# Out-projection stores of a two-layer encoder trunk, issued from POOL's queue in place of SP's

## The chip, the cores and the metric

The kernel runs on one core of a Trainium2 chip. Its engines are named as in the profile: PE is TensorE (matmuls; PEld are its weight loads), DVE is VectorE, ACT is ScalarE, POOL is GpSimd, and SP is SyncE, which here only issues DMAs. Each engine works through its own instructions in order. An instruction that waits (for another engine's result, for a buffer, for a DMA to land) holds up all that stand behind it on the same engine. A DMA is issued by one engine's queue and then carried out by 16 DMA engines that all queues share. The metric is device time in microseconds (us). Before the change the median of three runs is 2117.21 us (2113.16 to 2118.84).

## The reference, cut to what matters

A trunk of two layers works on 1024 tokens with 16 learned tokens in front (1040), 1024 channels, in float32. Each layer normalises, projects to four head groups of 512 channels (pooling, 2-D Fourier, bidirectional state-space scan "SSD", grouped-query attention), gates each, and projects the concatenation back:

```python
def reference(x, meta_tokens, norm_w, w_in, w_out, ...):
    h = jnp.concatenate([meta, x], axis=1)
    for i in range(DEPTH):
        hn = rmsnorm(h, norm_w[i])
        proj = jnp.einsum("bld,de->ble", hn, w_in[i])
        ...
        y_pool = multiscale_pool(u_pool, ...) * jax.nn.silu(g_pool)
        y_fft = fourier_mix(u_fft, fourier_w[i]) * jax.nn.silu(g_fft)
        y_ssd = ssd_mixer(xbc, z, dt_raw, ...)
        y_att = gqa_axial(q, k, v, ...) * jax.nn.silu(g_attn)
        mixed = jnp.concatenate([y_pool, y_fft, y_ssd, y_att], axis=-1)
        h = h + jnp.einsum("ble,ed->bld", mixed, w_out[i])
    return h[:, N_META:]
```

The last product, with `w_out`, is the out-projection. The change is in the code that adds its results to `h` and stores them.

## The kernel before, in words

All activations stand channel by channel: 128 channels on the partitions, tokens along the row, cut into three chunks (348, 346 and 346 tokens; in the second layer the first chunk loses the 16 learned tokens and has 332). For float32 accuracy each operand is split into a high part (cast on ACT, L128) and a low part (subtraction on DVE, L129), and each product takes three matmuls (L132, L133, L134).

The out-projection is not one product over 2048 channels. It is made in four passes, one per group of 512 channels, as soon as the group is ready: `outproj` is called for group 0 (pooling), then 1 (Fourier), then 3 (attention), then 2 (SSD, called the tail). Each pass reads `h` plus what earlier passes added from DRAM (hidden tensors, `hd` in the profile, or the input `xT`), adds its part, and writes the sum back to DRAM for the next pass; the last pass of the last layer writes `out`.

One pass has 8 blocks of 128 output channels times 3 chunks, 24 items. An item does this:

- SP loads the block of `h` to a small tile `ht` (L338). These tiles (`sms` in the profile) come from a ring of four buffers, which other steps use too: spilled projections (L239, L240), loads of group results (L325), the accumulator of the SSD's end (L950).
- TensorE makes 12 matmuls to a PSUM bank (`psmm`, or a spare bank `psy`).
- DVE adds the bank to `ht` in place (L352). In the attention group's pass (`pool=True`) ACT copies the bank to a second small tile (L349) and POOL adds (L350). In the tail of the first layer the sum goes to a tile that stays on chip as well (`sink`), since it is the next layer's input.
- SP stores the sum (L353).

That makes 24 stores for each of four groups and two layers, 192 in all. Once per block SP also loads the weights (L205, a ring of four buffers), which ACT and DVE split.

The passes don't run by themselves. Items are woven between the steps of other stages: the attention's last part (POOL adds to `acc` at L663 and L665), `fft_tables`, `fft_inner` (its inputs are loaded at L443 and L455, POOL clears tiles at L453 and L480), `fft_outer`, the gates, the SSD. How many items go to which stage is set by hand (the tables `FB`, `FW`, `TW`). The tile framework then schedules each engine's instructions from this program, so that a change of one instruction's engine can move others.

`fft_outer` matters for the change. It makes four sets of four matmul groups, each group with six matmuls against a cosine or sine table and one more at L518. POOL issues the DMA of each set's table (L499), and of one small table before (L493). The results of the first and third set are copied by ACT (L522), those of the second and fourth are combined by DVE (L524, L525). The gates are loaded by SP at L312, and ACT applies their silu at L306, ahead of the third set's copies. After this stage the SSD begins, with products at L790 and loads at L830 and L835.

Of the kernel before, what the change touches and what calls it, by code (L numbers as in the profile page):

```python
# [52 lines left out]
def hybrid_trunk(ctx: ExitStack, tc: tile.TileContext, io, out, depth=DEPTH):  # L53
    nc = tc.nc
# [42 lines left out]
    def big(dt=F32):  # L97
        return bigp.tile([128, SLOT], dt, name=nm("big"), tag="big", bufs=NBIG)
# [3 lines left out]
    def sm(tag="n", dt=F32):  # L102
        pool = phase["p"] if tag == "q" else smp
        return pool.tile([128, 348], dt, name=nm("sm" + tag), tag="sm" + tag, bufs=phase["q"] if tag == "q" else SMB[tag])
# [12 lines left out]
    def ps(tag):  # L117

        ring = [tag] * PSB[tag] + [x for x, t in zip(("y0", "y1", "y2"), phase["spare"]) if t == tag]
        turn[tag] = (turn[tag] + 1) % len(ring)  # L120
        x = ring[turn[tag]]
        return psp.tile([128, 512], F32, name=nm("ps" + x), tag=x, bufs=PSB.get(x, 1))
# [8 lines left out]
    def mm3(out_ps, ah, al, bh, bl, start, stop):  # L131
        nc.tensor.matmul(out_ps, ah, bh, start=start, stop=False)  # L132
        nc.tensor.matmul(out_ps, ah, bl, start=False, stop=False)  # L133
        nc.tensor.matmul(out_ps, al, bh, start=False, stop=stop)  # L134
# [58 lines left out]
    def wsplit(raws, cols=128):  # L193

        r = []
        for raw in raws:
            wh = wp.tile([128, 4, 128], F32R, name=nm("wh"), tag="wh", bufs=WB[1])
            wl = wp.tile([128, 4, 128], F32R, name=nm("wl"), tag="wl", bufs=WB[1])
            split(wh[:, :, :cols], wl[:, :, :cols], raw)
            r += [(wh[:, k, :cols], wl[:, k, :cols]) for k in range(4)]  # L200
        return r

    def wraw(src, cols=128):
        w = wp.tile([128, 4, 128], F32, name=nm("wr"), tag="wr", bufs=WB[0])
        nc.sync.dma_start(w[:, :, :cols], src)  # L205
        return w[:, :, :cols]
# [123 lines left out]
    def outproj(l, s, g, mixed, src, dst, chunks=(0, 1, 2), pool=False, sink=None):  # L330

        part = mixed()
        for d in range(8):
            w = wsplit([wraw(io["w2"][l, g, d])])
            for ci in chunks:
                c0, cw = s.ch[ci]
                ht = sm("s")[:, :cw]
                nc.sync.dma_start(ht, src(d, ci)[:, -cw:])  # L338
                p = ps("mm")
                for k in range(4):  # L340
                    mm3(p[:, :cw], *w[k], part(s, 0, k, ci), part(s, 1, k, ci), k == 0, k == 3)
                o = ht
                if sink is not None:
                    if len(sink) == d:
                        sink.append(big())
                    o = sink[d][:, c0:c0 + cw]
                if pool:
                    t = sm("s")[:, :cw]
                    nc.scalar.copy(t, p[:, :cw])  # L349
                    nc.gpsimd.tensor_tensor(o, ht, t, op=ALU.add)  # L350
                else:
                    nc.vector.tensor_tensor(o, ht, p[:, :cw], op=ALU.add)  # L352
                nc.sync.dma_start(dst(d, ci)[:, -cw:], o)  # L353
                yield


# [662 lines left out]
    for l in range(depth):  # L1019
# [29 lines left out]
        def early():  # L1049

            s.pm = load_mixed(s, "p")
            for _ in range(GP):
                yield
        fill2 = chain(early(), outproj(l, s, 0, lambda: s.pm, hsrc, d0), outproj(l, s, 1, lambda: s.fm, d0, d2), outproj(l, s, 3, lambda: s.am, d2, d1, pool=True))
        main = att_main(l, s, 3)
        run(weave((islice(main, LS + 3 * PC - 1), LS + 3 * PC - 1), (chain(*side), PS), (chain(fill, islice(fill2, GP + FB[0])), WF * (n + GP + FB[0]))))
# [23 lines left out]
        hsrc = by_rows(out, NM) if last else hidden()  # L1080
        sink = None if last else []
        tail = lambda chunks: outproj(l, s, 2, lambda: ssd_parts(s, chunks), d1, hsrc, chunks, sink=sink)
        fwd = ssd_fwd(l, s)
        n = 48 - FB[6] - FB[7]
# [119 lines left out]
```

## Time and profile before

| | before |
|---|---|
| runs, us | 2113.16, 2117.21, 2118.84 |
| profiled execution: own time | 2113.91 us |
| profiled execution: span in the profile | 2112.0 us |
| granted TensorE clock, mean | 0.981 |
| TensorE busy | 94% of the span |
| DVE, ACT, POOL busy | 66%, 48%, 17% |
| DMA packets of POOL's queue (software_dynamic), share of 16 engines | 1.7% |
| DMA packets of the other issuers' queue (hardware_dynamic) | 38.9% |

The span is the time between the first and the last instruction that the profiler recorded; the execution's own time is 1.9 us longer. A row such as `PE psmm L132 <- DVE sms L352: 9.2, 11, 2.1` reads: TensorE, at its instruction on line 132 that writes a tile `psmm`, stood for 9.2 us in 11 cases, at most 2.1 us, until DVE's instruction on line 352 that writes a tile `sms` had ended. `SPq` is SP's queue of DMA issues. Line 352 is the add, 353 the store, 338 the load of `h`. The clock column of the stage rows is the TensorE clock that was granted in that window as a share of full speed.

### The profile page before, as it was taken

Reading aid. Unit: us, or ns where it says so; the run is one execution under the profiler, and the core shown is the slowest. Engines: PE = TensorE matmul, PEld = TensorE weight load, DVE = VectorE, ACT = ScalarE, POOL = GpSimd, SP = SyncE. Lnnn points to the kernel's source line nnn. Section 1 sums busy time; section 2 is a strip of 40 time slices with the busy share of each in tenths; the row PEclk is TensorE's granted clock in tenths of the full one; section 3 lists DMA queues with packets and bytes.
Section 4 is the critical chain, followed back from the end, with each engine's and each line's share of the span. In section 5 each row is a group of like instructions: output and inputs, shape, how many; then the busy total and the mean of one; then the engine's idle time right before and its main releaser. Section 6 shows DMA issues by size and latency. Waiting matters only on the chain. (4 is left out here: it accounts for less than half of the span.)

```text
span 2112.0 us, 33087 instructions
## 1 busy us (share of the span) xinstructions
PE 1991.0 (94%) x11880; PEld 1744.1 (83%) x11880; DVE 1397.0 (66%) x2693; ACT 1012.7 (48%) x2192; POOL 369.0 (17%) x365
## 2 busy tenths in 40 slices
PE   6999999999999998998789999999999999989988
PEld 4898988688899777887779988876888995878877
DVE  5675546767665555799785755476676636477985
ACT  5544344453543546356465343436535425463562
POOL 2012122032120300013120121221312203000330
PEclk9999999999999998999899999999999999989999
DMA  4321221123232567766644221122122335877766
GB/s 139 101 75 60 67 65 57 42 74 98 92 126 97 172 207 234 203 182 186 176 123 121 68 67 55 59 61 69 65 96 98 116 117 153 248 219 198 195 180 182
DMA packets 164666, 260.99 MB, mean 124 GB/s; under 512 B 20938, under 2 KB 113678, under 8 KB 164502
## 3 DMA queue, kind: packets, MB, share of 16 engines
q1 hardware_dynamic: 161846, 249.56, 38.9%
q0 software_dynamic: 2656, 9.33, 1.7%
q8 instruction: 93, 1.52, 0.3%
q14 instruction: 71, 0.58, 0.1%
HBM read 182.92 MB, written 71.67 MB: 121 GB/s over the span
## 5 line engine op out<-in xcount | busy, mean ns | idle before, releaser
L132 PE MATMUL psmm<-big,wh 128*128 128x346 f32 (+2 forms) x1920 | 643.9, 336 | 35.3 <-ACT sms L349 12.7
L133 PE MATMUL psmm<-big,wh 128*128 128x346 f32 (+2 forms) x1920 | 628.7, 327 | 8.7 <-DVE big L129 5.6
L134 PE MATMUL psmm<-big,wl 128*128 128x346 f32 (+2 forms) x1920 | 624.6, 326 | 2.6 <-DVE wl L129 2.6
L132 PEld LDWEIGHTS psmm<-big,wh 128*128 128x128 f32 x1920 | 368.5, 192 | 84.5 <-issue 31.8
L133 PEld LDWEIGHTS psmm<-big,wh 128*128 128x128 f32 x1920 | 368.4, 192 | 17.9 <-DVE big L129 7.9
L134 PEld LDWEIGHTS psmm<-big,wl 128*128 128x128 f32 x1920 | 368.5, 192 | 5.9 <-DVE wl L129 4.3
L665 POOL TENSOR_TENSOR acc<-acc,pf 116x346 f32<-116x346 f32 (+5 forms) x216 | 221.0, 1036 | 672.9 <-ACT pf L655 537.9
L128 ACT CAST wh<-wr 128x512 fp32r<-128x512 f32 (+1 forms) x236 | 145.1, 616 | 265.2 <-PE psmm L133 182.7
L129 DVE TENSOR_TENSOR wl<-wr,wh 128x512 fp32r<-128x512 f32 x232 | 162.0, 703 | 123.0 <-ACT wh L128 121.8
L132 PE MATMUL psy<-big,wh 128*128 128x346 f32 (+2 forms) x672 | 221.2, 329 | 3.2 <-ACT big L128 2.5
L133 PE MATMUL psy<-big,wh 128*128 128x346 f32 (+2 forms) x672 | 217.3, 323 | 3.1 <-DVE big L188 2.0
L134 PE MATMUL psy<-big,wl 128*128 128x346 f32 (+2 forms) x672 | 216.5, 322 | 0.0
L655 ACT ACTIVATE pf<-psy 116x346 f32<-116x346 f32 (+4 forms) x288 | 125.4, 457 | 89.4 <-PE psy L653 88.2
L675 PE MATMUL pspv<-pf,vt 116*64 116x346 f32 (+5 forms) x864 | 165.5, 465 | 0.0
L665 DVE TENSOR_TENSOR acc<-acc,pf 116x346 f32<-116x346 f32 (+5 forms) x120 | 109.3, 911 | 75.5 <-ACT pf L655 51.0
L624 DVE TENSOR_REDUCE mx<-psy 116x1 f32<-116x346 f32 (+3 forms) x272 | 132.7, 511 | 17.3 <-PE psy L623 16.9
L132 PEld LDWEIGHTS psy<-big,wh 128*128 128x128 f32 x672 | 126.6, 188 | 15.2 <-issue 7.4
L133 PEld LDWEIGHTS psy<-big,wh 128*128 128x128 f32 x672 | 126.6, 188 | 6.9 <-DVE big L188 3.1
L134 PEld LDWEIGHTS psy<-big,wl 128*128 128x128 f32 x672 | 126.7, 189 | 0.8
L350 POOL TENSOR_TENSOR sms<-sms,sms 128x346 f32<-128x346 f32 (+2 forms) x48 | 61.9, 1292 | 355.3 <-DMA bb<-csd 230.6
L675 PEld LDWEIGHTS pspv<-pf,vt 116*64 116x64 f32 (+1 forms) x864 | 59.0, 136 | 61.7 <-issue 26.0
L352 DVE TENSOR_TENSOR sms<-sms,psmm 128x346 f32<-128x346 f32 (+2 forms) x104 | 52.8, 509 | 73.5 <-PE psmm L134 37.6
(293 smaller groups left out, 3273.0 us busy)
## 6 DMA issues: line engine op xcount, KB each, us to landing
wr<-w SPq DMA_DIRECT2D x248, 256.0 KB
sms<-hd SPq DMA_DIRECT2D x112, 173.0 KB
hd<-sms SPq DMA_DIRECT2D x96, 173.0 KB
bb<-csd SPq DMA_DIRECT2D x40, 338.0 KB
md<-big SPq DMA_DIRECT2D x24, 520.0 KB
gd<-sms SPq DMA_DIRECT2D x64, 173.0 KB
big<-gd SPq DMA_DIRECT2D x16, 520.0 KB
big<-md SPq DMA_DIRECT2D x16, 520.0 KB
```

Source lines behind the costliest of these rows:

```text
L128: nc.scalar.copy(hi, src)
L129: nc.vector.tensor_tensor(lo, src, f(hi), op=ALU.subtract)
L132: nc.tensor.matmul(out_ps, ah, bh, start=start, stop=False)
L133: nc.tensor.matmul(out_ps, ah, bl, start=False, stop=False)
L134: nc.tensor.matmul(out_ps, al, bh, start=False, stop=stop)
L350: nc.gpsimd.tensor_tensor(o, ht, t, op=ALU.add)
L352: nc.vector.tensor_tensor(o, ht, p[:, :cw], op=ALU.add)
L624: nc.vector.tensor_reduce(mx[:qn, q, e, ci:ci + 1], p[:qn, :cw], axis=AX.X, op=ALU.max)
L655: nc.scalar.activation(pf[:n, :cw], p[:n, :cw], AF.Exp, scale=0.125)
L665: eng.tensor_tensor(accs[c0, e][:n, :cw], accs[c0, e][:n, :cw], pf[:n, :cw], op=ALU.add)
L675: nc.tensor.matmul(hold["pv"][64 * e:64 * e + 64, :cw], s.vt[:n, k, v, :], pfs[e][:n, :cw], start=(k == 0), stop=(k == len(KTS) - 1))
```

## The change

One word changes in `outproj`: the store is issued from POOL's queue.

```diff
                 else:
                     nc.vector.tensor_tensor(o, ht, p[:, :cw], op=ALU.add)
-                nc.sync.dma_start(dst(d, ci)[:, -cw:], o)
+                nc.gpsimd.dma_start(dst(d, ci)[:, -cw:], o)
                 yield
```

All 192 stores move from SP's to POOL's queue, where each waits for its add. The scheduler then orders the other instructions anew. The numbers behind tile names tell tiles apart: an item's small tile, its bank and its sum have numbers close to each other.

On SP in the last tail (second layer, group 2), a piece of the difference: L338 loads `h` for an item, L205 loads weights, L893 loads a table of the SSD.

```order
 L205 DMA wr_21526<-w 128x512
 L338 DMA sms_21372<-hd_16517 128x346
 L205 DMA wr_21578<-w 128x512
-L353 DMA out<-sms_21315 128x332
 L205 DMA wr_21601<-w 128x512
-L353 DMA out<-sms_21332 128x346
-L353 DMA out<-sms_21355 128x332
 L338 DMA sms_21437<-hd_16516 128x332
-L353 DMA out<-sms_21372 128x346
 L338 DMA sms_21454<-hd_16517 128x346
```

The stores leave the queue, and the loads and weight loads stand directly behind each other.

On POOL in the first layer's Fourier stage, a piece of the difference: L493 and L499 are the tables of `fft_outer` (the tile 7973 is the second set's, 8051 the third's, 8123 the fourth's), L353 the stores of group 0.

```order
 L493 DMA big_7916<-dw 96x1048
 L499 DMA big_7918<-dl 128x1048
+L353 DMA hd_5729<-sms_8106 128x346
+L353 DMA hd_5727<-sms_8151 128x348
+L353 DMA hd_5728<-sms_8222 128x346
 L499 DMA big_7973<-dl 128x1048
+L353 DMA hd_5729<-sms_8259 128x346
+L353 DMA hd_5727<-sms_8282 128x348
 L499 DMA big_8051<-dl 128x1048
 L499 DMA big_8123<-dl 128x1048
```

The second set's table now stands behind three stores, the third's behind two more. The order in the second layer is alike.

On TensorE the items stand elsewhere around these sets. Before, the second set's first matmuls (`psxx_7975`) come after nine matmuls of the item with the bank 8261:

```order
L134 MATMUL psmm_8261<-big_7142,wl_8148 128x346
L132 MATMUL psmm_8261<-big_7143,wh_8147 128x346
L133 MATMUL psmm_8261<-big_7147,wh_8147 128x346
L134 MATMUL psmm_8261<-big_7143,wl_8148 128x346
L132 MATMUL psxx_7975<-big_7973,big_7871 128x262
L133 MATMUL psxx_7975<-big_7973,big_7871 128x262
```

Now they come after all of the next item's:

```order
L134 MATMUL psmm_8284<-big_7143,wl_8279 128x348
L132 MATMUL psmm_8284<-big_7144,wh_8278 128x348
L133 MATMUL psmm_8284<-big_7148,wh_8278 128x348
L134 MATMUL psmm_8284<-big_7144,wl_8279 128x348
L132 MATMUL psxx_7975<-big_7973,big_7871 128x262
L133 MATMUL psxx_7975<-big_7973,big_7871 128x262
```

Items stand about one item earlier against the transform's sets than before. In the order after, TensorE makes the whole item with the bank `psy_8224` (its sum is stored from the small tile 8222), one matmul of 8261, the first set, the other 11 of 8261, the 12 of 8284 (stored from 8282), the second set, ten of the next item, and the third set.

## The prediction

> **What bounds the kernel now.** I read the page's busy table first, then what TensorE waited for, then what SP's queue waited for, then the same waits stage by stage.
>
> ```profile
> PE 1991.0 (94%) x11880; PEld 1744.1 (83%) x11880; DVE 1397.0 (66%) x2693; ACT 1012.7 (48%) x2192; POOL 369.0 (17%) x365
> ```
>
> TensorE is busy for 1991 of 2112 us, so a change that leaves the matmuls alone can only win from the 121 us in which it stands. The waits of TensorE (line that waits, what ended it, total us, times, longest):
>
> ```profile
> PE psmm L132 <- ACT sms L349: 12.7, 11, 3.1
> PE psy L132 <- ACT big L522: 9.3, 2, 4.7
> PE psmm L132 <- DVE sms L352: 9.2, 11, 2.1
> ...
> PE psy L790 <- DVE sms L352: 4.0, 1, 4.0
> ...
> PE psmm L132 <- DVE big L352: 1.8, 2, 1.1
> ```
>
> L352 and L349 read an out-projection's sum out of PSUM. While they are late no bank comes free and TensorE stops. The four rows that name them make 12.7 + 9.2 + 4.0 + 1.8 = 27.7 us, 1.3% of the span: more than that the change cannot win directly. Why they are late stands in the waits of SP's queue:
>
> ```profile
> SPq L353 <- POOL sms L350: 99.1, 45, 7.2
> SPq L353 <- DVE sms L352: 98.2, 58, 9.3
> ...
> SPq L338 <- DMA hd<-sms: 89.0, 65, 5.4
> ...
> SPq L353 <- DVE big L352: 30.0, 18, 3.4
> ```
>
> SP stands in front of stores (L353) for 99.1 + 98.2 + 30.0 = 227 us, waiting for sums that aren't added yet, with loads (L338) queued behind. It also stands 89 us in front of loads whose buffer an earlier store is still reading. The first wait leaves SP with this change; the second stays.
>
> Where it matters, by stage (window, length, busy us of PE, PEld, DVE, ACT, POOL, granted clock, DMA share, GB/s): late pool group and attention group of layer 0, its SSD tail, the end of layer 1.
>
> ```profile
> 906.00:1010.00 104.00, 91.10 (x672) 83.93 (x672) 96.19 (x200) 63.84 (x170) 27.55 (x24) 0.98 0.68 184
> 1010.00:1085.00 75.00, 61.41 (x336) 55.53 (x334) 59.98 (x116) 33.14 (x78) 12.78 (x13) 0.91 0.63 179
> 2045.00:2112.00 67.00, 55.64 (x314) 52.15 (x314) 41.95 (x89) 16.83 (x39) 1.48 (x1) 0.91 0.65 183
> ```
>
> The waits on the sums in the windows 837 to 906, 1878 to 1945 and 2045 to 2112 (the first two are the second out-projection of each layer):
>
> ```profile
> PE psmm L132 <- DVE sms L352: 1.8, 3, 0.7
> ```
> ```profile
> PE psmm L132 <- DVE sms L352: 2.6, 2, 1.9
> ```
> ```profile
> PE psmm L132 <- DVE sms L352: 4.7, 6, 2.1
> ```
>
> **The change part by part.** The sums are made against the profiled execution: span 2112.0 and 1.9 us outside, 2113.9, which is 3.3 below the median of 2117.2. I apply the difference to the median.
>
> *What a store costs on each queue.* SP's store rows, then two POOL DMAs with their issue and landing times (L618 moves 256 to 260 KB, L499 524 KB; a store has 173 KB):
>
> ```profile
> L353 SPq DMA_DIRECT2D hd<-sms x144: 319/326/1044, 724.3 to 2046.5; - x144
> ```
> ```profile
> L618 POOL DMA_DIRECT2D big<-big x16: 509/547/687, 117.9 to 1542.9; - x16
> ...
> DMA to landing us min/median/max: 2.9/3.4/4.8
> ```
> ```profile
> L499 POOL DMA_DIRECT2D big<-dl x8: 537/541/554, 769.9 to 1839.3; - x8
> ...
> DMA to landing us min/median/max: 3.5/5.9/7.9
> ```
>
> The issue grows from 0.33 to about 0.55 us and moves off SP, where 192 × 0.33 = 63 us come free that TensorE never waited for. The landing of SP's stores is in the chain of waits of the last 50 us (start, length, piece):
>
> ```profile
> 2068.26 3.53 DMA out<-sms
> ...
> 2074.39 4.63 DMA sms<-hd
> ...
> 2079.68 2.64 DMA out<-sms
> 2082.33 4.58 DMA sms<-hd
> ```
>
> So an SP store lands in 2.6 to 3.5 us; from POOL no row shows one. The nearest is L618 in size, 2.9 to 4.8; I take its median 3.4 and keep 5.9 of L499 as the upper bound.
>
> *Last tail.* A buffer's round is: store waits for SP, lands, load lands, add. An add there, and what SP does after it; then three stretches of this stage (columns as above):
>
> ```profile
> 2071.19 0.51 DVE L352 TENSOR_TENSOR sms<-sms,psmm 128x346 f32<-128x346 f32 x1
> ...
> 2073.49 0.33 SPq L338 DMA_DIRECT2D sms<-hd  x1
> ...
> 2073.92 0.38 SPq L353 DMA_DIRECT2D out<-sms  x1
> ```
> ```profile
> 2076.00:2078.00 2.00, 1.26 (x8) 1.29 (x9) 1.53 (x3) 0.00 (x0) 0.00 (x0) 1.00 0.84 163
> 2078.00:2081.40 3.40, 3.06 (x12) 2.64 (x11) 2.26 (x5) 0.62 (x1) 0.00 (x0) 0.50 0.85 255
> ...
> 2095.00:2105.00 10.00, 10.00 (x64) 10.00 (x64) 4.71 (x9) 1.24 (x2) 0.00 (x0) 1.00 0.61 162
> ```
>
> The sum was ready at 2071.70 and its store left at 2073.92: 2.2 us lost because a load, itself waiting for a buffer, stood ahead of it. On POOL the store leaves at once. Undisturbed, a matmul takes 10.00 / 64 = 0.156 us (last stretch). The round has four buffers, so it has the time of four items of 12 matmuls, 7.5 us of TensorE. It was up to 2.2 + 3.5 + 4.6 + 0.5 = 10.8 and becomes 3.4 + 0.1 + 4.6 + 0.5 = 8.6. That still doesn't fit under 7.5, so of the 4.7 us a part stays. The stage also runs at a clock of 0.91, which costs 67 × 0.09 = 6 us against a full clock: behind a stretch with a gap of TensorE (1.26 busy of 2.00) the clock is 0.50 for 3.4 us. I take −4 (0 to −8).
>
> *Second out-projection, both layers.* The ceiling is 1.8 + 2.6 = 4.4; loads come earlier by the same argument: −3 (0 to −4.4).
>
> *Attention group (L349, L350).* There the add is on POOL, which also gets the store. Its waits, 906 to 1010 and 1945 to 2045:
>
> ```profile
> PE psmm L132 <- ACT sms L349: 8.9, 7, 3.1
> ```
> ```profile
> PE psmm L132 <- ACT sms L349: 3.8, 4, 1.9
> ```
>
> POOL's 24 adds took 27.55 us of 104 (row above), and 24 × 0.55 = 13 us come on top; POOL stays under 40%. SP no longer waits for these adds, but where two follow each other the second is now 0.55 us later and its load cannot start before. Earlier loads against later adds: 0 (−4 to +4).
>
> *Layer 0's SSD tail.* Sums go to tiles that stay, so buffers come free at the add: −1 of the 1.8 (0 to −1.8).
>
> *End.* The last store is on the path:
>
> ```profile
> 2108.06 0.52 DVE L352 TENSOR_TENSOR sms<-sms,psmm 128x346 f32<-128x346 f32 x1 [1.39 <-PE psmm L134]
> 2108.61 0.33 SPq L353 DMA_DIRECT2D out<-sms  x1
> ```
>
> From 2108.61 to 2112.0 are 3.4 us; POOL's bounds are 2.9 to 5.9: +0.5 (−0.5 to +2.5). The Trainium skill, "DMA: Bandwidth & Descriptors", section Specifications, gives about 1 us to the first byte from GpSimd's queue against 0.6 from SP's; that would make this term an estimated +0.4.
>
> *Fourier stages, both layers.* Here POOL also issues the tables (L499), and by the new order two of them stand behind stores that wait for adds. Before, they left when their buffer came free:
>
> ```profile
> 786.70 0.54 POOL L499 DMA_DIRECT2D big<-dl  x1 [16.25 <-PE psxx L474]
> 788.32 0.54 POOL L499 DMA_DIRECT2D big<-dl  x1 [1.07 <-PE psmm L134]
> ```
>
> ```profile
> L518 PE MATMUL psy<-big,big x3: 284/286/286, 794.0 to 796.6; 96*128 96x262 f32 x3
> ```
>
> The second table (tile 7973) now follows the add of item 8224: 0.52 + 0.07 for the hand-overs + 0.54 for the store = 1.1 us after the item's last matmul, and lands 3.5 to 7.9 later, at 4.6 to 9.0 (median 7.0). Between lie 24 matmuls (24 × 0.156 = 3.7) and four groups of the transform (the L518 row: three steps in 2.6 us, 0.86 each, 3.4): 7.1 us. So it is in time at the median and 1.9 late at worst. The third table follows the add of item 8284 in the same way: 7.0 at the median against 4 × 0.86 + 10 × 0.156 = 5.0, so 2.0 late. That is covered by a wait that is there anyway: three groups on, TensorE waits up to 4.7 us for ACT's L522, because ACT stands in front of the gates' silu until their loads are in:
>
> ```profile
> 804.96 1.08 ACT L306 ACTIVATE big<-big 128x1040 f32<-128x1040 f32 x1 [6.35 <-DMA big<-gd]
> ```
>
> I expect these loads within 1 us of before; if that cover went, 2 us a layer would show. I take +1 for the tables, +1 for transform inputs that SP now issues behind more loads of h, and −1 of the 4.0 us at L790, because its item's load no longer waits behind three stores, though ACT's casts hold TensorE nearly as long: +1 (−5 to +8).
>
> Sum: −4 − 3 + 0 − 1 + 0.5 + 1 = −6.5. On the median: 2110.7, say 2111. A measurement of this kernel can tell about 0.3% (6.3 us) from no change, so this lies on that edge.
>
> **The rivals.**
>
> *Slower: POOL's stores land late.* The round decides: what is left of it besides the landing is 0.1 + 4.6 + 0.5 = 5.2. Before, a round took between 2.6 + 5.2 = 7.8 and 10.8, in the middle 9.3. So from a landing of 9.3 − 5.2 = 4.1 us on the change loses. At L499's 5.9 a round is 11.1, 1.8 longer; I estimate that 14 rounds bind (6 in the last tail, 4 in each second out-projection): +25. At L618's worst, 4.8, it is 0.7 longer: +10. I take +11, near the lower, 2128. For it: the DMA engines are 63 to 85% busy there (stage rows and stretches above), so a landing can be long. Against: with 173 KB a store is nearer to L618.
>
> *No change.* What is won may pass to the next in line, above all to DVE, which is busy 96.19 of 104 us in the attention group's stage. Then only SP's 63 us of issue time are won, which nobody waited for: 2117. The 2.2 us between sum and store speak against it: they are order in the queue, not transfer. The Trainium skill, "DMA: Bandwidth & Descriptors", section "Issuing engines are not separate DMA queues", says that DMAs from any engine share the same 16 engines and that another issuer saves only issue time; by that rule this rival's time is the result.
>
> *Stores held while DVE runs.* If DVE's work keeps POOL from building a transfer, each store waits for part of an add-sized operation, 0.25 to 0.6 us (DVE was busy 41.95 of 67 us). Three terms shrink to −2, −1 and 0 and the Fourier stages cost +2: −1, 2116. Issues of 509 to 687 ns in L618's row leave little room for it. The Trainium skill, "SBUF — State Buffer", section "SBUF: two separate sides", describes this for DVE's two-port modes; no row here shows which operations use them.
>
> *Larger gain.* All rounds fit, and the half-clock stretches after these gaps go too: 12 of the 27.7 us and 3 of the clock's 6: −15, 2102.
>
> **How the numbers follow.** Forecast case 0.50, of it about half beyond 0.3%; larger gain 0.14; slower 0.23; no change 0.08; stores held 0.05. Faster 0.26 + 0.14 = 0.40, same 0.24 + 0.08 + 0.05 = 0.37, slower 0.23. The forecast's own range is 2105 to 2116 (−12 to −1.5). The whole range reaches from the larger gain with 5 us more, 2097, to the slower case at +12, 2129, leaving out the far ends of these two.
>
> **What the profile after would show.** Right: no store row on SP; the sums' waits of TensorE fall from 27.7 to about 18; POOL's store issues are 0.5 to 0.6 us with landings under 4.1; stores start within 0.1 us of their add; L499's third table is late by about 2 us under the wait for L522. Wrong: landings over 4.1, loads that wait longer for a store's landing than 89 us in all, a new wait of TensorE on tables in the transform, or adds at L350 that wait for POOL's own issues.

## The result and the profile after

| | before | after |
|---|---|---|
| median, us (runs) | 2115.45 (4) | 2136.61 (4) |
| lowest to highest, us | 2113.16 to 2118.84 | 2131.55 to 2144.05 |
| profiled execution: span | 2112.0 us | 2129.8 us |
| granted TensorE clock, mean | 0.981 | 0.973 |

The changed kernel is slower: ratio 1.0115, with a 95% interval of 1.0086 to 1.0145, or 21.2 us between the medians (whose quotient, 1.0100, lies inside the interval) and 17.8 us between the two profiled spans. The busy table after:

```profile
PE 1994.8 (94%) x11880; PEld 1749.5 (82%) x11880; DVE 1395.6 (66%) x2693; ACT 1012.7 (48%) x2191; POOL 463.2 (22%) x557
```

TensorE has the same 11880 matmuls and 3.8 us more busy time, so the lower clock did not lengthen its work by more than about that. POOL has 192 instructions more, the stores; ACT has one fewer, and the other counts are the same. So 14.0 of the 17.8 us are standing time of TensorE. Its waits after (columns as in the prediction):

```profile
...
PE psmm L132 <- ACT big L128: 9.1, 3, 3.6
PE psmm L132 <- DVE sms L352: 8.6, 8, 2.1
...
PE psy L132 <- ACT big L128: 8.2, 4, 3.6
PE psmm L132 <- ACT sms L349: 8.1, 8, 2.0
PE psy L132 <- DMA big<-dl: 7.8, 2, 4.1
...
PE psy L790 <- ACT big L306: 6.0, 5, 3.6
PE psmm L132 <- DVE big L352: 4.8, 3, 3.5
...
PE pssc L790 <- ACT big L306: 3.6, 2, 2.9
```

The waits on the sums did fall, to 8.6 + 8.1 + 4.8 = 21.5 us from 27.7; the 4.0 us at L790 that waited for a sum are gone. In their place TensorE waits for operands of the Fourier stages and of the SSD's start. The rows of before for the same kinds:

```profile
PE psy L132 <- ACT big L128: 4.7, 6, 1.9
PE psmm L132 <- ACT big L128: 3.5, 2, 1.9
...
PE pssc L790 <- ACT big L306: 1.5, 3, 0.6
```

ACT's casts (L128) held TensorE for 4.7 + 3.5 = 8.2 us and now for 17.3, the silu at L306 for 1.5 and now for 6.0 + 3.6 = 9.6, and the tables (`dl`), which have no row in before, for 7.8. Against these 7.8 stands a row that went: the 9.3 us for ACT's copies at L522. The stores themselves behave as the prediction assumed (POOL's rows for L353 and for the tables, L499, with time to landing):

```profile
L353 POOL DMA_DIRECT2D hd<-sms x144: 539/542/582, 725.3 to 2054.6; - x144
...
DMA to landing us min/median/max: 2.1/3.2/8.1
```
```profile
L499 POOL DMA_DIRECT2D big<-dl x8: 548/551/554, 786.6 to 1856.0; - x8
...
DMA to landing us min/median/max: 5.7/7.7/9.2
```

A store issues in 0.54 us and lands after 3.2 at the median. The tables land 7.7 after their issue, where the row of before had 5.9.

**By stage.** To see where the 17.8 us arise I cut both traces at the same matmuls of TensorE (for instance, the outer transform ends at the 16th matmul of L518), and took each stage's length after minus before. Items may stand in another stage now, so for each item matmul that a stage gained, 0.157 us (one such matmul undisturbed) were taken off, and put on for each that it lost. The last three columns are experiments that come below. A single cell can be off by some us: with group 0 alone on POOL the second layer's attention group, whose stores did not move there, differs by 4.7. What counts is a sign that returns in both layers and in several kernels.

| stage | length before | after | group 0 alone on POOL | group 0 back on SP | `z` late |
|---|---|---|---|---|---|
| inner transform, layer 0 | 33.3 | +4.8 | +3.3 | +1.3 | +4.3 |
| outer transform, layer 0 | 33.7 | +0.8 | +1.2 | −1.2 | −0.4 |
| SSD's start, layer 0 | 25.1 | +3.6 | +2.1 | 0.0 | +0.9 |
| inner transform, layer 1 | 42.3 | +3.6 | +4.4 | −0.2 | +4.8 |
| outer transform, layer 1 | 32.8 | −0.6 | +1.3 | −1.6 | −0.1 |
| SSD's start, layer 1 | 17.2 | +5.8 | +6.2 | +0.2 | +0.6 |
| late pooling and attention, layer 0 | 56.6 | −5.2 | −3.6 | −6.1 | −4.1 |
| last tail, to the last store's issue | 70.2 | −2.5 | −0.7 | +3.3 | −0.1 |
| from the last store's issue to the end | 3.4 | +6.5 | −0.2 | +2.6 | +6.5 |

After: +18.0 in the six Fourier and SSD rows, +6.5 at the end, −7.7 where the prediction hoped for gains, +1.0 in the rest.

**The Fourier stages.** SP's queue at the start of layer 0's inner transform, which has four input tiles (L443), first before, then after:

```profile
756.56 0.42 SPq L443 DMA_DIRECT2D big<-md  x1
...
760.56 0.43 SPq L443 DMA_DIRECT2D big<-md  x1
...
762.38 0.34 SPq L443 DMA_DIRECT2D big<-md  x1
...
767.23 0.42 SPq L443 DMA_DIRECT2D big<-md  x1
...
769.71 0.43 SPq L941 DMA_DIRECT2D z<-gd  x1
```
```profile
758.60 0.34 SPq L443 DMA_DIRECT2D big<-md  x1
...
762.27 0.42 SPq L941 DMA_DIRECT2D z<-gd  x1
762.75 0.50 SPq L443 DMA_DIRECT2D big<-md  x1
764.89 4.78 SPq L338 DMA_DIRECT2D sms<-xT  x2
...
771.57 0.33 SPq L443 DMA_DIRECT2D big<-md  x1
...
777.18 0.42 SPq L443 DMA_DIRECT2D big<-md  x1
```

The second input leaves 2.2 us later than before, the third and fourth 9.2 and 10.0; ahead of them two loads of `h` (L338) stand in the queue for 4.8 us. And the load of `z`, which only the SSD needs, has moved from behind all four inputs to ahead of the second. ACT in the same place, before and after (`z` gets its silu at L306, which needs a table load):

```profile
761.64 0.63 ACT L128 CAST big<-big 128x521 fp32r<-128x521 f32 x1 [3.53 <-DMA big<-md]
764.07 0.63 ACT L128 CAST big<-big 128x521 fp32r<-128x521 f32 x1 [1.80 <-DMA big<-md]
...
778.97 1.37 ACT L306 ACTIVATE z<-z 128x1392 f32<-128x1392 f32 x1
```
```profile
764.33 0.63 ACT L128 CAST big<-big 128x521 fp32r<-128x521 f32 x1 [6.14 <-DMA big<-md]
769.42 0.62 ACT L128 CAST wh<-wr 128x512 fp32r<-128x512 f32 x1 [4.47 <-PE psmm L133]
770.06 1.28 ACT L306 ACT_TABLE_LOAD   x1
771.36 1.37 ACT L306 ACTIVATE z<-z 128x1392 f32<-128x1392 f32 x1
772.63 0.61 ACT L128 CAST big<-big 128x521 fp32r<-128x521 f32 x1
```

Before, the casts of the first two inputs stood 2.4 us apart; now they are 8.3 us apart. Between them stand a cast of weights, which waited 4.5 us for TensorE, and `z`'s silu with its table load, 2.7 us. TensorE does not stand all this time: it makes items that were woven in for later (16 item matmuls more in the inner transform of layer 0, 21 of layer 1), and these are missing at the SSD's start, where TensorE then waits for ACT's silu and casts. The loss shows up some 60 us behind its cause.

The waits of SP's queue tell where the loads of `h` stand, first after, then a row of before that the prediction doesn't show (its other row was 89.0):

```profile
SPq L338 <- DMA hd<-sms: 212.5, 93, 13.2
...
SPq L338 <- POOL sms L350: 42.0, 19, 5.9
...
SPq L338 <- DMA out<-sms: 36.7, 18, 5.1
...
SPq L338 <- DVE big L352: 23.1, 13, 5.3
```
```profile
SPq L338 <- DMA out<-sms: 16.2, 12, 3.1
```

SP no longer waits for adds with the store; it waits longer with the load, for the landing of the store that still reads the buffer (212.5 + 36.7 = 249.2 us from 105.2) or for the add itself (65.1). All rows of L338 and L353 in this view make 354 us before and 348 after. The queue was not set free: the wait has moved one instruction on. POOL in layer 0's outer transform:

```profile
802.29 0.55 POOL L499 DMA_DIRECT2D big<-dl  x1 [0.28 <-issue]
806.83 0.54 POOL L353 DMA_DIRECT2D hd<-sms  x1 [3.99 <-DVE sms L352]
...
809.26 1.15 POOL L499 DMA_DIRECT2D big<-dl  x2
```

The tables stand behind stores that wait for adds. The one that left at 809.26 is what TensorE waits for at 817.48:

```profile
817.48 0.56 PE L132 MATMUL psy<-big,big 128*128 128x260 f32 x1 [4.14 <-DMA big<-dl]
```

Before, TensorE stood nearly as long in the same set, three groups later, for ACT's L522; after, that wait is gone:

```profile
812.65 0.58 PE L132 MATMUL psy<-big,big 128*128 128x260 f32 x1 [4.55 <-ACT big L522]
```

So the wait for the table took the place of another, and the rows of the outer transform in the stage table are +0.8 and −0.6.

**The end.** The last store and POOL's closing DRAIN, an instruction with which each engine ends (line 1200 is the kernel's end; the third number is the longest of the three, and it started at the first time given), then the DRAIN of before:

```profile
2119.90 0.54 POOL L353 DMA_DIRECT2D out<-sms  x1 [1.36 <-DVE sms L352]
```
```profile
L1200 POOLq DRAIN  x3: 46/93/9124, 2119.9 to 2129.5; - x3
```
```profile
L1200 POOLq DRAIN  x3: 46/102/8928, 2039.8 to 2111.7; - x3
```

From the last store's issue to the end it is 9.9 us, of which POOL's DRAIN takes 9.1, though the store has long landed (at 2122.3). Before, POOL's DRAIN began at 2039.8, behind POOL's last add, and ran hidden under 70 us of other work.

### The profile page after: what moved, and what is told of

It reads as the page before. It is cut to its first block, busy times and chain, and to the rows that moved or that the text cites. A ratio compares the mean times of both kernels' runs of the same rounds, so it can differ in the third digit from the quotient of the medians.

```text
span 2129.8 us, 33184 instructions
## 1 busy us (share of the span) xinstructions
PE 1994.8 (94%) x11880; PEld 1749.5 (82%) x11880; DVE 1395.6 (66%) x2693; ACT 1012.7 (48%) x2191; POOL 463.2 (22%) x557
## 5 line engine op out<-in xcount | busy, mean ns | idle before, releaser
L128 ACT CAST wh<-wr 128x512 fp32r<-128x512 f32 (+1 forms) x236 | 145.1, 616 | 273.8 <-PE psmm L133 180.2
L353 POOL DMA_DIRECT2D hd<-sms x144 | 78.9, 548 | 309.1 <-DVE sms L352 280.6
```

The lines of the kernel that those rows point to most:

```text
L128: nc.scalar.copy(hi, src)
L353: nc.gpsimd.dma_start(dst(d, ci)[:, -cw:], o)
```

## The experiments

Three theories for the loss. *Order*: group 0's stores make the scheduler and the queues put the Fourier stages' operands later, which costs TensorE about 9 us a layer. *End*: the DRAIN costs 6.5 us. *Landing* (the prediction's slower rival): stores from POOL land late, and cost in every pass. All ratios are against the kernel before on the same chip; "against after" is the quotient of two such ratios.

### The last store alone on POOL

```diff
-                nc.sync.dma_start(dst(d, ci)[:, -cw:], o)
+                (nc.gpsimd if (l, g, d, ci) == (depth - 1, 2, 7, 2) else nc.sync).dma_start(dst(d, ci)[:, -cw:], o)
```

> The kernel before with only its very last store (second layer, group 2, last block and chunk) issued from POOL. Theory (the end): in the profile of before POOL's closing DRAIN takes 8.9 us, at 2039.8, under the last 60 us of other work; in the profile after it takes 9.1 us behind the last store and everything waits for it, 9.9 us from the last store's issue to the end against 3.4. One store is enough for that: +6 to +7 us on before, and a DRAIN of about 9 us behind it. Rival 1 (many stores): the drain is long because 192 stores went through POOL's queue, so one store leaves it at 1 to 3 us: +0 to +2. Rival 2 (landing): only the longer way of a POOL store counts: 0 to +0.5.

Ratio 1.0009 (0.999 to 1.0028). The DRAIN:

```profile
L1200 POOLq DRAIN  x3: 46/102/3628, 2116.6 to 2120.7; - x3
```

With one store there it takes 3.6 us and the end is 4.4 us instead of 3.4. That a DRAIN behind the last store takes 9 us whatever was queued fell.

### Group 0 back on SP, and group 0 alone on POOL

The first is made from after, the second from before:

```diff
-                nc.gpsimd.dma_start(dst(d, ci)[:, -cw:], o)
+                (nc.gpsimd if g != 0 else nc.sync).dma_start(dst(d, ci)[:, -cw:], o)
```
```diff
-                nc.sync.dma_start(dst(d, ci)[:, -cw:], o)
+                (nc.gpsimd if g == 0 else nc.sync).dma_start(dst(d, ci)[:, -cw:], o)
```

> The changed kernel with the 48 stores of group 0 back on SP; these are the ones woven into the attention's end and the Fourier stages. Theory (three places: Fourier stages +8 to +9 us a layer, the end +6.5, the first layer's tail +5, the first layer's attention group -8): the Fourier stages lose their new waits, TensorE's wait for the tables goes from 7.8 to 0, and the time falls by 12 to 17 us against the changed kernel, to 2120 to 2125. Rival (every store costs alike, because a landing from POOL is longer): a quarter of the stores, so a quarter of the loss, 4 to 6 us.

> The kernel before with only the 48 stores of group 0 issued from POOL; all others stay on SP. Theory (the loss is made where group 0's items are woven into the Fourier stages): +15 to +20 us on before, with TensorE waiting about 8 us for the tables and with inputs, gates and casts late as in the changed kernel. Rival (the loss is a sum of small prices of all stores and of the end): a quarter of it, +5.

With group 0 back on SP and the other 144 stores on POOL: 2117.24 us, ratio 1.0012 (0.9993 to 1.0032). With only group 0's 48 stores on POOL: 2133.31 against 2111.74 us, ratio 1.0101 (1.0079 to 1.0122). So 48 stores, with nothing at the end (the DRAIN is hidden there), cost as much as all 192, 21.6 us, and 144 stores cost nothing that can be measured. That settles *Landing*: it would have cost with the 144. But those 144 gained nothing that can be measured either, and the waits on sums did not fall. TensorE with group 0 back on SP:

```profile
PE psmm L132 <- DVE sms L352: 10.7, 9, 3.5
...
PE psmm L132 <- ACT sms L349: 9.0, 8, 2.1
...
PE psmm L132 <- DVE big L352: 4.8, 3, 3.5
...
PE psy L790 <- DVE sms L352: 4.1, 1, 4.1
```

That is 28.6 us, where before had 27.7. The stage table agrees on the loss, the six Fourier and SSD rows making +18.5 with group 0 alone on POOL and −1.5 with it back on SP. ACT with group 0 alone on POOL has the silu of `z` where after has it, ahead of the second input's cast:

```profile
763.29 0.63 ACT L128 CAST big<-big 128x521 fp32r<-128x521 f32 x1 [5.32 <-DMA big<-md]
...
770.54 1.36 ACT L306 ACTIVATE z<-z 128x1392 f32<-128x1392 f32 x1
771.81 0.61 ACT L128 CAST big<-big 128x521 fp32r<-128x521 f32 x1
```

### Group 3 alone on POOL

```diff
-                nc.sync.dma_start(dst(d, ci)[:, -cw:], o)
+                (nc.gpsimd if g == 3 else nc.sync).dma_start(dst(d, ci)[:, -cw:], o)
```

> The kernel before with only the 48 stores of group 3 (the attention group, added on POOL) issued from POOL. In the run with group 0 back on SP the first layer's attention group ended 9 us earlier against before than it began, and the SSD tail behind it lost 8 of them. Theory a (the tail's own stores on POOL lost it): with the tail's stores on SP the 9 us of the first layer stay: -5 to -9 us on before. Theory b (what is won in the attention group is waited for again in the tail, whose end is set by other work): 0 (-2 to +2).

2113.86 us, ratio 1.0012 (0.9994 to 1.0031). The attention group, where POOL's adds meet POOL's stores, neither gains nor loses.

### Which of group 0's stores

Group 0 has 8 blocks of three stores per layer. In after, the first five blocks' stores go back to SP, so that mostly those are left on POOL that run beside the outer transform and the SSD's start:

```diff
-                nc.gpsimd.dma_start(dst(d, ci)[:, -cw:], o)
+                (nc.sync if g == 0 and d < 5 else nc.gpsimd).dma_start(dst(d, ci)[:, -cw:], o)
```

> The changed kernel with the first five of eight blocks of group 0's stores (15 of 24 items in each layer, up to the end of the inner transform) on SP; the other nine, beside the outer transform, stay on POOL, as do all other groups. SP's order in the inner transform is then that of before; the second table stands behind stores on POOL as in the changed kernel. Theory (two halves: inputs of the inner transform late by SP's order and by POOL's clearing of tiles behind stores, about 4 us a layer; tables and gates of the outer transform late, about 5 a layer): 8 us below the changed kernel, about 2128. Rival 1 (all of it the tables and gates): 0 to -3. Rival 2 (all of it the inner transform, and the rest follows): -15 to -20.

2123.87 us, ratio 1.0055 (1.0034 to 1.0075): 0.6% against after (0.24 to 0.96), some 13 us, came back. `z` stands late again here (its silu at 781.49). By the stages of the table above, the three rows of layer 0 are +1.5, +0.1 and +0.3, those of layer 1 +0.1, +0.5 and +1.9, +4.4 in all, where after has +18.0. The second table still stands behind three stores and the third behind two, so most of what costs in these stages comes from the stores up to the end of the inner transform.

### `z` late

In after, the first load of `z` is ordered behind the last input of the inner transform, and its silu behind this stage's small copies. These are orders for the scheduler, not waits (`after_(a, b)`, a helper not printed here, puts `a` behind `b`):

```diff
-            nc.sync.dma_start(t[rows, :n], src)
+            s.zin = nc.sync.dma_start(t[rows, :n], src)
...
-                        nc.scalar.copy(o[64:64 + k, cs], p[r:r + k])
+                        s.zact = nc.scalar.copy(o[64:64 + k, cs], p[r:r + k])
...
+        if ci == 0:
+            after_(zd, s.zin)
+        silu_([z[:, :, :cw]], s.zact if ci == 0 else None)
```

> The changed kernel, all 192 stores on POOL, with one order put back: in each layer the SSD's first load of its gate z (L941 of the changed kernel, 0.7 MB on SP) comes after the last input of the inner transform, and its silu on ACT after the inner transform's small copies, where both stood before. In the changed kernel's order they stand ahead of the second input and its cast on ACT. Theory (this jump, and not POOL's work, is the inner half of the loss): 8 to 13 us below the changed kernel, that is 1.003 to 1.008 of before; the second input's cast comes within 3 us of the first one's as before, and not 8 us later. Rival 1 (POOL: its clearing of tiles waits behind stores): 0 to -2. Rival 2 (SP's loads of h, which wait for stores to land, ahead of the inputs): 0 to -4.

2133.16 us, ratio 1.0073 (1.0046 to 1.0101), 0.42% (0.02 to 0.82) or about 9 us against after; by the medians alone it is 0.2% or 4 us, so little more than the sign is safe. The stage table shows where: the six Fourier and SSD rows fall from +18.0 to +10.1, the SSD's start goes from +3.6 and +5.8 to +0.9 and +0.6, and TensorE makes nearly as many items in each stage as before (one more, in place of 16 and 21). The inner transform keeps +4.3 and +4.8. ACT there:

```profile
766.01 0.63 ACT L128 CAST big<-big 128x521 fp32r<-128x521 f32 x1 [5.28 <-DMA big<-md]
770.26 0.63 ACT L128 CAST big<-big 128x521 fp32r<-128x521 f32 x1 [3.62 <-DMA big<-md]
```

The two casts are 4.3 us apart, and what ACT waits for is the input itself: the loads that SP issues behind loads of `h`.

### The inputs first

So in the kernel with `z` late the four input loads go to the start of the inner transform. The same edit was made in before, as a control (without `s.zin`, which is for `z`):

```diff
+        ins = [big() for _ in range(4)]
+        for t, k in zip(ins, (0, 2, 1, 3)):
+            s.zin = nc.sync.dma_start(t[:, :HALF + 1], s.md["r"][k])
+        ins = iter(ins)
...
-            t, r = big(), big(F32R)
-            nc.sync.dma_start(t[rows, :n], src)
+            t, r = next(ins), big(F32R)
```

> The changed kernel, all stores on POOL, with z put back as in the earlier run and, besides, the four inputs of the inner transform loaded at its start one behind the other on SP, so that no load of h, which waits for a store to land, stands between them. Theory (what z left of the inner half, 4 to 5 us a layer by TensorE's timeline, is inputs behind such loads): 6 to 9 us below the run with z alone (1.0073 of before), that is 1.003 to 1.005; the second input's cast within 2 us of the first's. Rival (POOL's clearing of tiles behind stores, or the stores themselves): 0 to -2, 1.006 to 1.008.

> Control: the kernel before with the four inputs of the inner transform loaded at its start. Theory: before, the inner transform lost 1 to 2 us a layer to inputs, so -1 to -3 us (0.9985 to 1). Rival: inputs first is a gain of its own as large as in the changed kernel, -6 or more.

With `z` late and inputs first: 2121.99 us, ratio 1.0028 (1.0012 to 1.0044), 0.45% or 9 us against `z` late alone. But the control gains as well, more than was expected: 2110.71 us, ratio 0.9975 (0.9958 to 0.9992). So about half of the 9 us is what this edit brings to before too. The other half, 0.20% or 4 us, would be loss undone, but its interval is −0.16 to 0.56%: it is not shown to differ from nothing. Both edits together leave 0.28% of the 1.15%, about 6 us, with a DRAIN at the end that still takes 9.1; against the control, which has the same inputs, they leave 0.53%.

### The tables early

Here each table of the outer transform is asked for one set earlier, so that it stands ahead of the stores (`TP = 0` becomes `TP = 1`): in after, in before as a control, in the kernel with `z` late, and in before with the inputs first.

```diff
-    TP = 0
+    TP = 1
```

> The changed kernel with each table of the outer transform issued one set earlier (TP = 1): the second table goes ahead of the three stores that it stood behind, the third takes the second's old place. All stores stay on POOL. Theory a (POOL's own queue: tables behind stores): TensorE's wait for tables, 4.1 and 3.7 us, goes, and the time falls by 4 to 8 us against the changed kernel. Theory b (SP's order: transform inputs and the gates' loads behind loads of h that wait for a store's landing): the table wait goes, but ACT, held by the gates' silu until 819, holds TensorE instead at the same place, and the time falls by 0 to 2 us only.

> The kernel before with each table of the outer transform issued one set earlier (TP = 1), as a control for the run that did so in the changed kernel and won about 7 us. Theory: before, no table was waited for, so this is 0 (-2 to +2); the 7 us were a wait that the stores had made. Rival: earlier tables are a gain of their own, -4 to -8.

> The changed kernel with z put back as in the run beside it and with tables one set earlier (TP = 1) as well. Theory (two causes in the Fourier stages, z ahead of the inputs and tables behind stores, and a third at the end): what is left on before is the end, about 4 to 6 us, less the 4 us that TP = 1 won in the kernel before: 0.997 to 1.003. Rival (other prices of all stores remain): over 1.005.

> The version that the runs point to: the kernel before, stores on SP, with inputs at the start of the inner transform and tables one set earlier. The tables alone gave 0.9972. Theory (the two waits stand at different places and add up): 0.995 to 0.997. Rival (the DMAs collide, or the gates' silu then holds TensorE anyway): 0.998 or above.

In after: 2129.78 us, ratio 1.0068 (1.0045 to 1.0091), 0.47% against after. That looked like the price of tables behind stores. The control says otherwise: before with it takes 2107.55 us, ratio 0.9972 (0.995 to 0.9995). So 0.28% is its own, and 0.19% (−0.24 to 0.62) is left for the wait that the stores made: not shown to differ from nothing. In the kernel with `z` late: 2128.74 us, ratio 1.0054 (1.0034 to 1.0073), where 0.997 to 1.003 was expected: the two edits do not remove all. Nor do two gains add up: before with the inputs first and the tables early takes 2114.41 us, ratio 1.0008 (0.999 to 1.0026). The fastest versions are before with early tables (0.9972) and before with the inputs first (0.9975), which these runs don't tell apart, and both store from SP.

### POOL's clearing of tiles

In after, POOL clears a tile of the inner transform (L453) at 771.05, before at 739.35, for it now stands behind stores. The clearing (L453, L480) moves to DVE:

```diff
-        nc.gpsimd.memset(f(r)[0:65], 0.0)
+        nc.vector.memset(f(r)[0:65], 0.0)
...
-                    nc.gpsimd.memset(f(o)[:, 512:1024], 0.0)
+                    nc.vector.memset(f(o)[:, 512:1024], 0.0)
```

> The changed kernel with the clearing of tiles in the inner transform (L453, L480) on DVE in place of POOL, so that it no longer waits behind stores on POOL. All stores stay on POOL and the gate z stays ahead of the second input. Theory (the jump of z): no difference from the changed kernel, 1.009 to 1.013 of before. Rival (POOL's clearing behind stores makes the inner transform late): 5 to 12 us below it.

2137.33 us, ratio 1.0123 (1.0082 to 1.0163): no gain on after is to be seen, with an interval of ±0.4%. This was tried with `z` early only.

### The end

In after, the last chunk's eight stores go from SP, and POOL's DRAIN begins earlier. In the second kernel only 107 stores are on POOL, none of group 0 among them, which with POOL's 26 other DMAs (16 at L618, 8 at L499, 2 at L493) makes 133:

```diff
-                nc.gpsimd.dma_start(dst(d, ci)[:, -cw:], o)
+                (nc.gpsimd if (l, g, ci) != (depth - 1, 2, 2) else nc.sync).dma_start(dst(d, ci)[:, -cw:], o)
```
```diff
-                nc.gpsimd.dma_start(dst(d, ci)[:, -cw:], o)
+                (nc.gpsimd if g > 1 or (l, g) == (1, 1) and 3 * d + ci > 12 else nc.sync).dma_start(dst(d, ci)[:, -cw:], o)
```

> The changed kernel with the last eight stores (second layer's tail, last chunk) on SP. They start about 15 us before the end, so that POOL's closing drain of 9 us lies beside them. Theory (the end): from the last store to the end 3.4 us in place of 9.9, -6 to -7 us against the changed kernel. Rival (the drain isn't what waits; the longer landing is): 0 to -1 us.

> The changed kernel with only 107 stores on POOL: groups 2 and 3, and the last eleven of group 1 in the second layer; with the 26 DMAs that POOL issues anyway it is 133 in all. One look at POOL's closing DRAIN behind the last store. In the profiles so far it lasted 3.4 and 3.6 us after 26 and 27 DMAs, 6.7 and 7.2 after 74, 5.2 after 170, 6.7 after 188, 8.5 after 210, 9.1 after 218. Theory 1 (it grows with the count from the last multiple of 128 on): 133 is 5 beyond, so 1 to 2 us. Theory 2 (it grows with the count alone, with scatter): 5 to 7 us. Theory 3 (it is chance): anything between 3 and 9.

With the last eight on SP the end is 3.3 us again, 6.6 shorter than after. Yet the time is 2135.05 us, ratio 1.0100 (1.0074 to 1.0127), 0.15% or 3 us against after, with an interval of −0.25 to 0.55%. Whether the 6.6 us came through can't be told from these runs. The second kernel was run once, at 2117.63 us, for its DRAIN.

The DRAINs right behind a store of the last tail, by the number of DMAs that POOL had issued in the run:

| DMAs from POOL | 27 | 133 | 170 | 188 | 210 | 218 |
|---|---|---|---|---|---|---|
| DRAIN, us | 3.63 | 3.58 | 5.21 | 6.67 | 8.47 | 9.12 |

From 170 on the DRAIN grows by (9.12 − 5.21) / 48 = 0.081 us per DMA, and that gives 6.68 at 188 and 8.47 at 210. It isn't the number alone. With group 3 alone on POOL, at 74 DMAs, it took 6.68 behind a store; in before, at 26 and with no store near it, 8.9; in three other kernels with all stores on SP, also at 26, 3.4 to 3.5. The 1 to 2 us expected at 133, from a count that starts anew after 128, missed. What sets the length stays open.

## Why the prediction was wrong

**What was right.** The store's own prices: 0.54 us on POOL, landing at 3.2 where 3.4 was taken. The turning point of the slower rival, 4.1, was not reached at the median, and no cost of landing is in the runs. The kernel did become slower, but not by that rival's mechanism; that its 2128 lies near the 2136.61 is luck. POOL's adds in the attention group neither gain nor lose (0 expected; ratio 1.0012 with group 3 alone). For the third set's table the working said 2.0 us late a layer, under the wait for L522. TensorE stood up to 4.1 us for it, and the cover held all the same: 7.8 us for tables stand where 9.3 for L522 stood, and the outer transform has +0.8 and −0.6.

**The step that failed: "The first wait leaves SP with this change; the second stays."** The first wait, 227 us in front of stores, did leave. The second did not stay: loads that waited 89.0 us (105.2 with those behind stores to `out`) wait 249.2 for landings and 65.1 for adds, 348 us in all at the two lines where 354 were before. SP runs ahead to the next load of `h` and stands there, with all that is behind it. Longer waits for landings were among the prediction's own signs of being wrong. Two parts of the sum rested on this step, and both came out wrong.

- The gains. The stores outside group 0 were forecast at −4 − 3 − 1 + 0.5 = −7.5. With them alone on POOL the runs show +0.12%, 2.5 us, with an interval of −1.5 to +6.8, and waits on the sums of 28.6 us against 27.7. In after they are 21.5, near the 18 that were named as a sign, but with the 144 alone that fall is not there. The last tail has −2.5 there, where −4 was expected, and +3.3 with group 0 back on SP, so this can't be told from scatter. The rule of the Trainium skill, "DMA: Bandwidth & Descriptors", section "Issuing engines are not separate DMA queues", that another issuer saves only issue time, agrees with these 144 stores. With the other 48 the measurement differs: they cost 1.0%.
- The Fourier stages. The prediction put "+1 (−5 to +8)" there, of it "+1 for transform inputs that SP now issues behind more loads of h", for both layers together. The trace shows +18.0, the experiment with group 0 alone on POOL +21.6 us of time.

On how the Fourier loss is made up the runs show this:

- The inputs did not cost 1 us: three of them left SP 2.2, 9.2 and 10.0 us later, behind the loads of `h`. With `z` put back the inner transform keeps +4.3 and +4.8, and ACT waits for these inputs; with the stores of group 0's first five blocks on SP it has +1.5 and +0.1. Moving the inputs ahead gave 4 us more than in the control, which is not clear of nothing, so how much of the 9 us the inputs make is not shown.
- A term is missing from the sum. The order was read at the stores and the tables only. On ACT and SP the scheduler also moved `z`, by 7.4 us on SP and from behind the transform's copies to ahead of the second cast on ACT. Putting `z` back gave about 9 us (4 by the medians), with the SSD's start back at +0.9 and +0.6; in the stage rows that is 8 of the 18. The prediction saw that items "stand about one item earlier" and took that for free. These items are what TensorE does at the next wait; made early, they are missing there.

**The second step: the end.** "+0.5 (−0.5 to +2.5)" was priced by a store's landing. It was +6.5 in the profile, since the last instruction was not the landing but POOL's DRAIN, whose row in before was hidden 70 us ahead of the end. That the DRAIN is there is shown; that the whole 6.5 us count in the time is not, since taking them away gave 3 us, in an interval that holds 0 and 6.6.

**What stays open.** What sets the DRAIN's length; how the inner transform's rest is made up; where the gain of the shorter end went; and why repairs in pairs gain less than their sum.

## What to carry to other kernels

Before moving one instruction to another engine's queue, compare the order of all engines, and look for instructions that nobody needs soon and that now stand ahead of some that are needed at once: here the load and silu of `z`, not the stores themselves, made 8 of the 18 us in the stage rows. Filler work has a use: where TensorE makes it early, ask which later wait it was covering. And an engine with hidden closing work should not be given the kernel's last instruction without counting that work at the end; a control, the same repair made in the kernel before, tells a repaired loss from a gain that was there anyway.

## What the runs showed of the hardware

POOL's closing DRAIN took from 3.4 to 9.1 us. Right behind the last tail's stores it grew from 5.2 us at 170 DMAs from POOL to 9.1 at 218, though in the profile after the last of them landed 2.4 us after its issue; the number alone doesn't set it, for before had 8.9 us at 26. A store of 173 KB from POOL landed at 2.1, 3.2 and 8.1 us (least, median, most), at the median no later than the two stores from SP, 2.6 and 3.5. Its issue took 539 to 582 ns beside a DVE that was busy 66% of the span, so the issue was not held while DVE ran; whether a long landing was, no run here shows.
